# Sixteen tokens of a dense expert block moved to the gathers, and the gathers dealt over all rows

## The chip, the cores and the metric

The kernel runs on 1 core of one Trainium2 chip. The metric is the device time of one execution in microseconds (us), as the median of several runs. The engines are called PE (TensorE matmul; PEld is its weight load), DVE (VectorE), ACT (ScalarE), POOL (GpSimd) and SP (SyncE, which here only issues DMAs).

## The reference

One transformer layer over 512 tokens of width 1024: an adaptive norm, a token mixer (two linear-attention branches), a second norm, and then an expert layer that is most of the time here. Cut to that layer:

```
q   = (xb @ wq).reshape(P, 8, 2, 128)               # P = 128 tokens of a block
sc  = einsum('phzd,hznd->phzn', q, subkeys)         # 2 x 128 keys per head
sv, si = top_k(sc, 16); top_s, top_c = top_k(sums of the 16 x 16 pairs, 16)
experts = si0 * 128 + si1 at top_c                  # 16 of 16384 experts per head
gate = softmax(top_s)
ue, ve = u_tab[experts], v_tab[experts]             # 8 heads x 16 = 128 experts a token
act = gelu(einsum('pd,phkd->phk', xb, ue)) * gate
out = einsum('phk,phkd->pd', act, ve)
```

There are 16384 experts, with a u row and a v row of 1024 floats each, and every token uses 128 of them.

## The kernel before

The 512 tokens are four blocks of 128. **Blocks 0 to 2 go the dense way.** The experts are cut into 128 rows of 128. For each row `i`, `scores(i)` loads 128 x 1024 words of u (`raw<-in_ut`), splits them into a rounded high part `whi` (ACT) and a rest `wlo` (DVE), and multiplies all 384 tokens with them on PE: 8 slices of the width x 3 products = 24 matmuls into the bank `hg`, each over `ND` = 384 token columns (`dhi`, `dlo`). ACT takes the gelu (`ga`). `value_parts(i)` loads and splits the v row (`raw<-in_uv`), multiplies `ga` with the gates of this row (`g`, read back from the DRAM tensor `gd`) and splits the product into `ah` (ACT) and `al` (DVE). `value_sum` adds the row to the three blocks' sums `y` in PSUM: 3 blocks x 2 halves x 3 products = 18 matmuls over 512 columns.

The first 32 rows' scores (`AHEAD`) are taken early, while the gates are still being made, and wait in the DRAM tensor `sd`; they come back as `gr`. So in `dense()` a row under 29 has 18 matmuls, and a later one 42, since it makes the scores of row `i + LEAD` as well.

**Gates.** `route()` takes a block's top 16 of 16 (DVE). `scatter(b, ...)` turns the choices into the dense matrix `gd`, 16 tokens in a turn of its loop over `q`: POOL and DVE make one-hot rows `oj` and `oi`, ACT multiplies gates in, PE multiplies `oj` by `oi` per token (128x128 matmuls, `gd<-oi,oj`), and ACT copies four tokens' results from PSUM into `stage`, one word per token at steps of 16 words.

**Block 3 goes the gathered way.** `gather_block` runs 128 steps; step `c` has POOL issue one indirect DMA that fetches, for each of the 128 tokens, the u and v row of its `c`-th expert (1 MB, five buffers `rows`). DVE takes the dot product with `h2g` (one 128x1024 operation), ACT the gelu, DVE multiplies the gate in and adds the v rows to `acc` (another 128x1024 operation). The steps are dealt among the rows: `run(dense(), ga_)` takes a step of `gather_all()` at each yield of `dense()`. `gather_all()` first ends the route of block 3, so the first yields go to it.

The program is written in this order, and a scheduler in the build settles the order on each engine; engines and the SP queue then work strictly in that order. `back_norm` is the norm ahead of the routes of blocks 2 and 3; its `sink` has POOL copy block 2's columns into `dhi` and `dlo`, PE transpose block 3's, and ACT copy them to `h2g`.

Of the kernel before, what the change touches and what calls it, by code (L numbers as in the profile page):

```python
# [45 lines left out]
NGS = 5  # L46
NST = 4
ADA = (12, 2)
ND = 384
AHEAD = 32  # L50
LEAD = 3
RING = 6
# [14 lines left out]
def mixer_peer_kernel(ctx: ExitStack, tc: tile.TileContext, x, ws, ada, wba, vecs, rows, skt, uv, ut, out, dbg=None):  # L67
# [270 lines left out]
    def pb4(pp, i):  # L338
        return pp[:, i * P:(i + 1) * P]
# [437 lines left out]
    def expert_index(sel):  # L777
        ef = wk.tile([P, PH, 16], F32, tag="lo", name="ef", bufs=1)
        nc.vector.scalar_tensor_tensor(ef, sel[0], 128.0, sel[1], op0=ALU.mult, op1=ALU.add)
        ei = gat.tile([P, PH * 16], I32, tag="ei", name="ei")  # L780
        nc.vector.tensor_copy(ei, f2(ef))
        return ei

# [126 lines left out]

    routes = []
# [5 lines left out]

    def back0(mg):
        hh, hl = dhi[:, :, 0:256], dlo[:, :, 0:256]
        yield from back(0, mg, (dhi[:, :, P:], dlo[:, :, P:]), hh, hl)  # L920
        yield from route(hh, hl, nc.vector, gat, routes)

    xc = load_x(0)
# [72 lines left out]


    den = ctx.enter_context(tc.tile_pool(name="den", bufs=1, **RT))
    h2g = den.tile([P, D], F32, name="h2g")
# [30 lines left out]
    def scatter(b, sel, gate, npool, pool, bufs, tags):  # L1030

        cols = []
        for n, src in (("ti", sel[0]), ("tj", sel[1]), ("tg", gate)):
            pp = bank("tr")
            nc.tensor.transpose(pp[:, 0:P], f2(src), ident)
            c = sct.tile([P, P], F32, tag=n, name=n, bufs=2)
            nc.scalar.copy(c, pp[:, 0:P])
            cols.append(c)
        ti, tj, tg = cols
        for q in range(P // 16):  # L1040
            sg = sct.tile([P, P, 16], F32, tag="stage", name="stage", bufs=2)
            for q4 in range(4):
                pp = bank(tags[q4 % len(tags)])
                t0 = q * 16 + q4 * 4
                oj4 = pool.tile([P, 4, P], F32, tag="oj", name="oj", bufs=bufs)
                oi4 = pool.tile([P, 4, P], F32, tag="oi", name="oi", bufs=bufs)
                for a in range(4):
                    (nc.gpsimd if a < npool else nc.vector).tensor_scalar(oj4[:, a, :], iof, tj[:, t0 + a:t0 + a + 1],  # L1048
                                                                      None, op0=ALU.is_equal)
                if q4 % 2:  # L1050
                    for a in range(4):
                        t = t0 + a
                        nc.vector.tensor_scalar(oi4[:, a, :], iof, ti[:, t:t + 1], tg[:, t:t + 1],
                                                op0=ALU.is_equal, op1=ALU.mult)
                else:
                    nc.vector.tensor_tensor(oi4, iof[:, None, :].to_broadcast([P, 4, P]),
                                            ti[:, t0:t0 + 4, None].to_broadcast([P, 4, P]), op=ALU.is_equal)
                    for a in range(4):
                        nc.scalar.mul(oj4[:, a, :], oj4[:, a, :], tg[:, t0 + a:t0 + a + 1])
                for a in range(4):  # L1060
                    last["pe"] = nc.tensor.matmul(pb4(pp, a), oj4[:, a, :], oi4[:, a, :], start=True, stop=True)  # L1061
                nc.scalar.copy(sg[:, :, q4 * 4:q4 * 4 + 4].rearrange("p i t -> p t i"),
                               pp.rearrange("p (t i) -> p t i", t=4))
            nc.sync.dma_start(gd[:, b * P // 16 + q], sg)
            yield

# [51 lines left out]
    def value_parts(i):  # L1118
        vh, vl = split_load(uv[i * P:(i + 1) * P, D:2 * D])
        if i % 8 == 0:  # L1120
            g = d3.tile([P, ND // 16, 8, 16], F32, tag="g", name="g", bufs=2)
            for b in range(ND // P if i == 0 else 1):
                q = slice(8 * b, 8 * b + 8) if i == 0 else slice(0, ND // 16)
# [9 lines left out]
        ah = d3.tile([P, ND], F32R, tag="ah", name="ah", bufs=2)  # L1133
        al = d3.tile([P, ND], F32R, tag="al", name="al", bufs=2)
        nc.scalar.copy(ah, a)
        last["lo"] = nc.vector.tensor_sub(al, a, ah)  # L1136
        return ah, al, vh, vl

    def value_sum(i, b, hf, ah, al, vh, vl):
# [2 lines left out]
        return mm3(yacc[b][:, d], ah[:, c], al[:, c], vh[:, d], vl[:, d], i == 0, i == P - 1)  # L1142


    def gather_block(h2, gate, ei, d3):
        acc = d3.tile([P, D], F32, tag="acc", name="acc")
        gf = f2(gate)
        r, g = {}, {}
        for c in range(NHK + LAG + 1):
            if c < NHK:  # L1150
# [11 lines left out]
            if 0 <= k < NHK:  # L1162
# [12 lines left out]
    def finish(b, y, gf, d3):  # L1175
# [32 lines left out]

    def gather_all():

        yield from rt
        ei = expert_index(routes[GB][1])
        c_hq.close()
        c_wr.close()
        rows_ = ctx.enter_context(tc.tile_pool(name="rows", bufs=1, reuse_waits="tile"))
        done.append(rows_)
        done.append((yield from gather_block(h2g, routes[GB][0], ei, rows_)))
# [72 lines left out]
```

## Time and profile before

| | |
|---|---|
| time, median of 3 runs | 1899.74 us (1898.4 to 1901.0) |
| the profiled execution's own time | 1898.62 us |
| its span in the trace | 1896.7 us |
| PE busy | 1844.5 us, 97% of the span |
| DVE, ACT, POOL busy | 83%, 51%, 22% |
| DMA traffic | 459.45 MB, 242 GB/s over the span |

The span lies 1.9 us under the execution's own time, and that 1.1 us under the median. "Busy" PE time counts overlapping matmuls, so that the spacing of matmul starts is read from the timeline. The stages in time: mixers to about 600 us, gates and early scores to 934, rows under 29 to 1061, later rows to 1885, then the last norm.

### The profile page before, as it was taken

How to read it: one execution, taken by the hardware profiler on the slowest of the kernel's cores; microseconds unless marked ns; L12 is line 12 of the kernel's file. 1: busy time of each engine (PE TensorE's matmuls, PEld its weight loads, DVE VectorE, ACT ScalarE, POOL GpSimd, SP SyncE). 2: the span in 40 equal slices, each digit the busy share in tenths (PEclk: the TensorE clock that was granted, in tenths of full speed). 3: DMA queues.
4: the chain of work that ended last, by engine and by line, in shares of the span. 5: the costliest groups of instructions: out<-in, count | busy, mean ns of one | idle time of the engine just before them, and what ended most of it. 6: DMA issues, size and time to landing. Idle time of an engine off the chain costs nothing.

```text
span 1896.7 us, 31316 instructions
## 1 busy us (share of the span) xinstructions
PE 1844.5 (97%) x11441; PEld 1708.1 (90%) x11441; DVE 1565.9 (83%) x3422; ACT 972.9 (51%) x1726; POOL 421.5 (22%) x433
## 2 busy tenths in 40 slices
PE   7999989999998999999999999999999999999997
PEld 7999978999998899999977898998998989989896
DVE  6889966989999989999766977887787778887855
ACT  6778634676655788787433333333333333333332
POOL 1000000000000788884100322122211221222100
PEclk9999989999999999999999999999999999999999
DMA  9556734543355556658998998988998998889833
GB/s 321 187 169 198 234 113 156 162 136 95 123 163 175 183 166 211 212 193 265 312 317 256 369 359 307 335 296 310 313 324 300 327 323 289 324 303 331 297 123 111
DMA packets 160521, 459.45 MB, mean 242 GB/s; under 512 B 12528, under 2 KB 78192, under 8 KB 140912
## 3 DMA queue, kind: packets, MB, share of 16 engines
q1 hardware_dynamic: 141936, 323.23, 51.7%
q0 software_dynamic: 18432, 134.23, 18.7%
q8 instruction: 90, 1.47, 0.3%
q14 instruction: 63, 0.52, 0.1%
HBM read 420.71 MB, written 36.70 MB: 241 GB/s over the span
## 4 chain that ended last, share of the span: by engine, by line
PE 91%; ACT 3%; DMA 2%; DVE 2%; POOL 1%; issue 1%; SPq 0%; DVEq 0%; POOLq 0%; ACTq 0%
PE hg L208 9%; PE hg L209 9%; PE hg L207 9%; PE y L208 9%; PE y L209 9%; PE y L207 9%; PE pj L207 8%; PE pj L208 8%; PE pj L209 8%; PE gd L1061 3%; PE hg L543 1%; POOL oj L1048 1%; PE gd L453 1%; PE gd L447 1%; PE pj L1061 1%; DMA adaw<-in_ada 1%
## 5 line engine op out<-in xcount | busy, mean ns | idle before, releaser
L1014 DVE TENSOR_TENSOR wlo<-raw,whi 128x1024 fp32r<-128x1024 f32 x256 | 313.3, 1224 | 124.4 <-ACT whi L1013 124.3
L1013 ACT CAST whi<-raw 128x1024 fp32r<-128x1024 f32 x256 | 267.8, 1046 | 246.4 <-PE y L209 224.4
L209 PE MATMUL hg<-dhi,whi 128*128 128x384 f32 x1024 | 347.9, 340 | 0.0
L207 PE MATMUL hg<-dlo,whi 128*128 128x384 f32 x1024 | 347.9, 340 | 0.0
L208 PE MATMUL hg<-dhi,wlo 128*128 128x384 f32 x1024 | 347.7, 340 | 0.0
L1152 POOL DMA_INDIRECT rows<-in_uv,ei x128 | 167.0, 1304 | 739.4 <-DVE acc L1160 573.1
L208 PE MATMUL y<-whi,al 128*128 128x512 f32 x768 | 304.8, 397 | 1.9 <-DVE al L1136 1.8
L209 PE MATMUL y<-whi,ah 128*128 128x512 f32 x768 | 304.4, 396 | 0.0
L207 PE MATMUL y<-wlo,ah 128*128 128x512 f32 x768 | 295.8, 397 | 0.0
L1048 POOL TENSOR_SCALAR oj<-iof,tj 128x128 f32<-128x128 f32 x256 | 218.7, 871 | 49.7 <-PE gd L1061 32.6
L203 DVE TENSOR_TENSOR wlo<-raw,whi 128x1024 fp32r<-128x1024 f32 x160 | 195.2, 1221 | 31.0 <-ACT whi L202 30.7
L202 ACT CAST whi<-raw 128x1024 fp32r<-128x1024 f32 x160 | 167.3, 1048 | 89.9 <-PE pj L209 62.4
L1027 ACT ACTIVATE ga<-hg 128x384 f32<-128x384 f32 x128 | 63.0, 493 | 276.6 <-PE hg L209 276.4
L208 PEld LDWEIGHTS hg<-dhi,wlo 128*128 128x128 f32 x1024 | 192.2, 188 | 4.2
L207 PEld LDWEIGHTS hg<-dlo,whi 128*128 128x128 f32 x1024 | 192.2, 188 | 4.1
L209 PEld LDWEIGHTS hg<-dhi,whi 128*128 128x128 f32 x1024 | 192.2, 188 | 0.1
L208 PEld LDWEIGHTS y<-whi,al 128*128 128x128 f32 x768 | 144.6, 188 | 35.0 <-DVE al L1136 4.4
L209 PEld LDWEIGHTS y<-whi,ah 128*128 128x128 f32 x768 | 144.5, 188 | 34.6
L207 PEld LDWEIGHTS y<-wlo,ah 128*128 128x128 f32 x768 | 144.6, 188 | 32.0 <-issue 1.0
L1165 DVE SCALAR_TENSOR_TENSOR rows<-rows,h2g 128x1024 f32<-128x1024 f32 x128 | 153.8, 1220 | 0.4 <-DMA rows<-in_uv,ei 0.4
L207 PE MATMUL pj<-wlo,hh 128*128 128x256 f32 x448 | 128.9, 288 | 5.0 <-ACT gsig L627 2.1
L209 PE MATMUL pj<-whi,hh 128*128 128x256 f32 x448 | 128.1, 286 | 0.0
(748 smaller groups left out, 3875.4 us busy)
## 6 DMA issues: line engine op xcount, KB each, us to landing
raw<-in_ws SPq DMA_DIRECT2D x160, 512.0 KB, 3.8
raw<-in_ut SPq DMA_DIRECT2D x128, 512.0 KB, 5.0
raw<-in_uv SPq DMA_DIRECT2D x128, 512.0 KB, 6.5
adaw<-in_ada SPq DMA_DIRECT2D x48, 512.0 KB, 5.2
gd<-stage SPq DMA_DIRECT2D x24, 1024.0 KB, 4.8
g<-gd SPq DMA_DIRECT2D x15, 1536.0 KB, 12.6
sd<-ga SPq DMA_DIRECT2D x32, 192.0 KB, 4.1
gr<-sd SPq DMA_DIRECT2D x32, 192.0 KB, 5.5
```

The source lines that it names most:

```text
L202: nc.scalar.copy(hi, w)
L203: nc.vector.tensor_sub(lo, w, hi)
L207: nc.tensor.matmul(o, lh, rl, start=start, stop=False, **kw)
L208: nc.tensor.matmul(o, ll, rh, start=False, stop=False, **kw)
L209: return nc.tensor.matmul(o, lh, rh, start=False, stop=stop, **kw)
L1013: nc.scalar.copy(hi, w)
L1014: nc.vector.tensor_sub(lo, w, hi)
L1027: nc.scalar.activation(a, o[:, :ND], AF.Gelu)
L1048: (nc.gpsimd if a < npool else nc.vector).tensor_scalar(oj4[:, a, :], iof, tj[:, t0 + a:t0 + a + 1], None, op0=ALU.is_equal)
L1061: last["pe"] = nc.tensor.matmul(pb4(pp, a), oj4[:, a, :], oi4[:, a, :], start=True, stop=True)
L1152: nc.gpsimd.indirect_dma_start(out=r[c], out_offset=None, in_=uv, in_offset=bass.IndirectOffsetOnAxis(ap=ei[:, c:c + 1], axis=0))
L1165: dot = nc.vector.scalar_tensor_tensor(u, u, 1.0, h2, op0=ALU.mult, op1=ALU.mult, accum_out=s)
```

## The change

`ND` becomes 368: the last 16 tokens of block 2 leave the dense matmuls of the scores, the gelu, the gates (`scatter` of block 2 makes 7 turns instead of 8) and `sd`, `gr`, `g`, `ga`. In `ah` and `al` their 16 columns are zeros that are set once, so the 18 value matmuls keep their shape. The 16 tokens x 128 experts are gathered instead: 2048 pairs are spread over 128 partitions as 8 groups of 16 tokens, so that 16 more gather steps do them. For this `sink` makes a tile `xr` that repeats the 16 tokens' columns 8 times (POOL), transposes it (PE) and copies it to `h2x` (ACT); 16 small DMAs on SP spread the expert numbers (`eix`) and gates (`gx`); and after the 16 steps four matmuls with `pick_x` (a matrix of ones and zeros) add the eight groups' sums `accx` into block 2's `y`.

The copy of `scatter` into `stage` now writes runs of four words and reads PSUM at steps of 128 words. The route of block 3 ends ahead of the first row, and the gather steps are dealt from row 1 on: one at every odd row under 29, then one or two at each row, three extra in seven rows (before: from row 20 on, one extra in three rows).

```diff
-ND = 384
+NX = 16
+NG = P // NX
+ND = 384 - NX
...
             if p:
-                nc.gpsimd.tensor_copy(dhi[:, c, 2 * P:], hh[:, c, 0:P])
-                nc.gpsimd.tensor_copy(dlo[:, c, 2 * P:], hl[:, c, 0:P])
+                nc.gpsimd.tensor_copy(dhi[:, c, 2 * P:], hh[:, c, 0:P - NX])
+                nc.gpsimd.tensor_copy(dlo[:, c, 2 * P:], hl[:, c, 0:P - NX])
+                xr_ = thp.tile([P, 2, P], F32, tag="xr", name="xr", bufs=1)
+                nc.gpsimd.tensor_copy(xr_.rearrange("p a (g t) -> p a g t", t=NX),
+                                      h32[:, :, None, P - NX:P].to_broadcast([P, 2, NG, NX]))
                 pp = bank("hg")
                 for a in range(2):
                     nc.tensor.transpose(pb4(pp, a), h32[:, a, P:], ident)
-                nc.scalar.copy(h2[:, j * 256:(j + 1) * 256], pp[:, 0:256])
+                    nc.tensor.transpose(pb4(pp, 2 + a), xr_[:, a, :], ident)
+                for n in range(2):
+                    nc.scalar.copy(h2[n][:, j * 256:(j + 1) * 256], pp[:, n * 256:(n + 1) * 256])
...
-        for q in range(P // 16):
+        for q in range((P - NX if b == GB - 1 else P) // 16):
...
-                nc.scalar.copy(sg[:, :, q4 * 4:q4 * 4 + 4].rearrange("p i t -> p t i"),
-                               pp.rearrange("p (t i) -> p t i", t=4))
+                nc.scalar.copy(sg[:, :, q4 * 4:q4 * 4 + 4], pp.rearrange("p (t i) -> p i t", t=4))
...
+    for dst, src in ((eix, expert_index(routes[GB - 1][1])), (gx, f2(routes[GB - 1][0]))):
+        for g in range(NG):
+            nc.sync.dma_start(dst[g * NX:(g + 1) * NX, :], src[P - NX:P, g * NX:(g + 1) * NX])
     run(first)
-    run(gates(2, NP[1], hold, 4, ("pj", "gd", "pj", "pj")))
+    run(gates(2, NP[1], hold, 4, ("pj", "gd", "pj", "pj")), rt)
+    run(rt)
...
-            if i >= 20 or i % 2:
+            if i >= AHEAD - LEAD or i % 2:
                 yield
-            if i >= AHEAD - LEAD and i % 3 == 0:
+            if i >= AHEAD - LEAD and i % 7 in (0, 2, 5):
                 yield
...
-        yield from rt
-        ei = expert_index(routes[GB][1])
...
+        x = yield from gather(h2g[1], gx, eix, NX, "accx")
+        hi = st.tile([P, D], F32R, tag="whi", name="whi")
+        lo = st.tile([P, D], F32R, tag="wlo", name="wlo")
+        nc.scalar.copy(hi, x)
+        nc.vector.tensor_sub(lo, x, hi)
+        for hf in range(2):
+            d = slice(hf * 512, hf * 512 + 512)
+            for t in (lo, hi):
+                nc.tensor.matmul(yacc[GB - 1][:, d], pick_x, t[:, d], start=False, stop=False)
+        done.append((yield from gather(h2g[0], f2(routes[GB][0]), ei, NHK, "acc")))
```

Two places show how instructions move. The first is POOL at the norm ahead of the routes (`back_norm`), whose copies stand among the one-hot rows `oj` of the gates. Before:

```order
L126 TENSOR_TENSOR rsn<-rs,mhalf 128x2
L1048 TENSOR_SCALAR oj<-iof,tj 128x128 x9
L903 COPY dhi<-thi 128x2x128
L1048 TENSOR_SCALAR oj<-iof,tj 128x128 x3
L904 COPY dlo<-tlo 128x2x128
L1048 TENSOR_SCALAR oj<-iof,tj 128x128 x3
L903 COPY dhi<-thi 128x2x128
L904 COPY dlo<-tlo 128x2x128
L903 COPY dhi<-thi 128x2x128
```

The same place with the change (L908 is the new copy):

```order
L128 TENSOR_TENSOR rsn<-rs,mhalf 128x2
L1055 TENSOR_SCALAR oj<-iof,tj 128x128 x9
L908 COPY xr<-h_8224 128x256
L905 COPY dhi<-thi 128x2x112
L1055 TENSOR_SCALAR oj<-iof,tj 128x128 x3
L906 COPY dlo<-tlo 128x2x112
L1055 TENSOR_SCALAR oj<-iof,tj 128x128 x3
L905 COPY dhi<-thi 128x2x112
L908 COPY xr<-h_8247 128x256
L906 COPY dlo<-tlo 128x2x112
L1055 TENSOR_SCALAR oj<-iof,tj 128x128 x6
```

Between one `xr` and the next there now stand six `oj`, and `xr` has one buffer. The second place is DVE in the rows under 29, where a dot product of a gather has its first operand from `rows`. Before, the first dot product comes behind the 23rd `al`:

```order
L1014 TENSOR_TENSOR wlo<-raw,whi 128x1024
L1132 TENSOR_TENSOR gr<-gr,g 128x384
L1136 TENSOR_TENSOR al<-gr,ah 128x384
L1165 SCALAR_TENSOR_TENSOR rows,gs__12642<-rows,h2g 128x1024
L1132 TENSOR_TENSOR gr<-gr,g 128x384
L1014 TENSOR_TENSOR wlo<-raw,whi 128x1024
```

With the change the first one comes behind the eighth `al`, and this is the piece around the fourth:

```order
L1159 TENSOR_TENSOR al_11846<-gr,ah_11845 128x368
L1188 SCALAR_TENSOR_TENSOR rows,gs__12319<-rows,h2x 128x1024
L1021 TENSOR_TENSOR wlo<-raw,whi 128x1024
L1156 TENSOR_TENSOR gr<-gr,g 128x368
L1193 TENSOR_TENSOR gg__12321<-gg__12321,gx 128x1
L152 TENSOR_SCALAR adac<-adaw,cond 128x512
L1183 SCALAR_TENSOR_TENSOR accx<-rows,gg__12321,accx 128x1024
L1156 TENSOR_TENSOR gr<-gr,g 128x368
L158 SCALAR_TENSOR_TENSOR adac<-adaw,cond,adac 128x512
L1159 TENSOR_TENSOR al_11844<-gr,ah_11843 128x368
```

From there on every second `al` has one gather step beside it, through all rows under 29; before, from the 23rd on, every `al` had one. By the end of the order the last dot product stands behind the 125th `al` (before: the 120th).

## Rows read from the trace of the kernel before

**Rows 1.** The page, first part: busy time, share of the span, instructions.

```profile
PE 1844.5 (97%) x11441; PEld 1708.1 (90%) x11441; DVE 1565.9 (83%) x3422; ACT 972.9 (51%) x1726; POOL 421.5 (22%) x433
```

**Rows 2.** Windows by stage: busy time of each engine, PEclk, DMA share, GB/s.

```profile
600.00:680.00 80.00, 72.61 (x527) 67.77 (x525) 71.64 (x154) 54.95 (x109) 56.92 (x70) 0.94 0.49 161
680.00:900.00 220.00, 218.03 (x1577) 215.47 (x1576) 209.61 (x788) 176.83 (x327) 166.10 (x198) 1.00 0.66 219
1060.00:1100.00 40.00, 40.00 (x198) 35.67 (x197) 38.12 (x56) 15.35 (x27) 14.59 (x10) 1.00 1.03 397
1100.00:1800.00 700.00, 700.00 (x3482) 631.86 (x3481) 558.34 (x775) 251.12 (x443) 138.77 (x108) 1.00 0.88 315
```

**Rows 3.** Timeline of PE in a later row: start, duration, instruction.

```profile
1301.64 0.33 PE L207 MATMUL hg<-dlo,whi 128*128 128x384 f32 x1
...
1305.88 0.39 PE L207 MATMUL y<-wlo,ah 128*128 128x512 f32 x1
...
1310.08 0.34 PE L207 MATMUL hg<-dlo,whi 128*128 128x384 f32 x1
```

**Rows 4.** Timeline of PE elsewhere: 33 matmuls of 256 columns, and 128-column ones.

```profile
103.36 0.28 PE L207 MATMUL pj<-hl,whi 128*128 128x256 f32 x1
...
107.32 0.28 PE L207 MATMUL pj<-hl,whi 128*128 128x256 f32 x1
...
805.68 1.28 PE L1061 MATMUL gd<-oi,oj 128*128 128x128 f32 x10
```

**Rows 5.** Groups by line and form, PEld and DVE, 1050 to 1800 us.

```profile
L208 PEld LDWEIGHTS hg<-dhi,wlo 128*128 128x128 f32 x697 | 130.8, 188 | 3.8
...
L1014 DVE TENSOR_TENSOR wlo<-raw,whi 128x1024 fp32r<-128x1024 f32 x179 | 219.1, 1224 | 91.8 <-ACT whi L1013 91.8
L1165 DVE SCALAR_TENSOR_TENSOR rows<-rows,h2g 128x1024 f32<-128x1024 f32 x121 | 145.3, 1220 | 0.4 <-DMA rows<-in_uv,ei 0.4
...
L1132 DVE TENSOR_TENSOR ga<-ga,g 128x384 f32<-128x384 f32 x87 | 48.5, 557 | 43.0 <-ACT ga L1027 42.8
L1136 DVE TENSOR_TENSOR al<-ga,ah 128x384 fp32r<-128x384 f32 x86 | 47.5, 552 | 5.4 <-ACT ah L1135 5.4
...
L1160 DVE SCALAR_TENSOR_TENSOR acc<-rows,gg__13464,acc 128x1024 f32<-128x1024 f32 x1 | 1.3, 1287 | 0.0
```

**Rows 6.** Groups by line, gates and norm: ACT in 600 to 900, POOL in 640 to 700.

```profile
L1062 ACT COPY stage<-gd 128x512 f32<-128x512 f32 x72 | 76.0, 1073 | 12.0 <-PE gd L1061 11.9
...
L675 ACT COPY qt<-pj 128x512 f32<-128x512 f32 x8 | 4.7, 591 | 2.0 <-PE pj L209 2.0
...
L1048 POOL TENSOR_SCALAR oj<-iof,tj 128x128 f32<-128x128 f32 x58 | 51.0, 895 | 6.1 <-PE gd L1061 6.1
L904 POOL CAST dlo<-tlo 128x256 fp32r<-128x256 f32 x4 | 2.3, 563 | 0.0
```

**Rows 7.** One line, L1061: what the scatter's matmuls waited for (us, times).

```profile
  ACT oj L1059: 13.2, 21
  POOL oj L1048: 3.3, 6
```

**Rows 8.** The tile `y`, 927 to 1062: its matmuls and their wait (us, times).

```profile
L207 PE MATMUL y<-wlo,ah x177: 391/397/798, 934.1 to 1061.6; 128*128 128x512 f32 x177
...
  DVE al L1136: 5.9, 9
```

**Rows 9.** DMA, 925 to 1060: packets and rate, gathers issued.

```profile
DMA packets 20818, 40.97 MB, mean 303 GB/s; under 512 B 1333, under 2 KB 14388, under 8 KB 19654
...
rows<-in_uv,ei POOLq DMA_INDIRECT x10, 8.9
```

**Rows 10.** DMA, 1100 to 1800: the gathers' queue, and their count.

```profile
q0 software_dynamic: 15864, 115.47, 43.8%
...
rows<-in_uv,ei POOLq DMA_INDIRECT x108, 8.3
```

**Rows 11.** The chain that ended last, at the last rows.

```profile
1875.94 0.25 PE y L209
...
1877.37 0.51 PE y L208
```

More of the change, by code (lines that the diff above doesn't have):

```diff
@@ L779, in expert_index @@
         nc.vector.scalar_tensor_tensor(ef, sel[0], 128.0, sel[1], op0=ALU.mult, op1=ALU.add)
-        ei = gat.tile([P, PH * 16], I32, tag="ei", name="ei")
+        ei = gat.tile([P, PH * 16], I32, tag="ei", name="ei", bufs=2)
         nc.vector.tensor_copy(ei, f2(ef))
@@ L919, in back0 @@
         hh, hl = dhi[:, :, 0:256], dlo[:, :, 0:256]
-        yield from back(0, mg, (dhi[:, :, P:], dlo[:, :, P:]), hh, hl)
+        yield from back(0, mg, (dhi[:, :, ND - 256:], dlo[:, :, ND - 256:]), hh, hl)
         yield from route(hh, hl, nc.vector, gat, routes)
@@ L998, in mixer_peer_kernel @@
     den = ctx.enter_context(tc.tile_pool(name="den", bufs=1, **RT))
-    h2g = den.tile([P, D], F32, name="h2g")
+    h2g = [den.tile([P, D], F32, name=n) for n in ("h2g", "h2x")]
     c_th = ctx.enter_context(ExitStack())
@@ L1098, in mixer_peer_kernel @@
         next(first, None)
+    eix = gat.tile([P, NX], I32, name="eix")
+    gx = gat.tile([P, NX], F32, name="gx")
+    for dst, src in ((eix, expert_index(routes[GB - 1][1])), (gx, f2(routes[GB - 1][0]))):
+        for g in range(NG):
+            nc.sync.dma_start(dst[g * NX:(g + 1) * NX, :], src[P - NX:P, g * NX:(g + 1) * NX])
     run(first)
-    run(gates(2, NP[1], hold, 4, ("pj", "gd", "pj", "pj")))
+    run(gates(2, NP[1], hold, 4, ("pj", "gd", "pj", "pj")), rt)
+    run(rt)
+    ei = expert_index(routes[GB][1])
     run(ahead)
     c_hd.close()
+    c_hq.close()
+    c_wr.close()
     c_sc.close()
@@ L1108, in mixer_peer_kernel @@
     psv = ctx.enter_context(tc.tile_pool(name="psv", bufs=1, reuse_waits="tile", space=PSUM))
-    yacc = [psv.tile([P, D], F32, name=f"y{b}") for b in range(ND // P)]
+    yacc = [psv.tile([P, D], F32, name=f"y{b}") for b in range(GB)]
+    s32 = d3.tile([P, P], F32, name="s32")
+    nc.vector.memset(s32, 0.0)
+    nc.vector.tensor_reduce(s32[:, P - NX:], ident.rearrange("p (g t) -> p t g", g=NG), axis=AX.X, op=ALU.add)
+    pick_x = d3.tile([P, P], F32R, name="pick_x")
+    nc.vector.tensor_copy(pick_x, s32)
+    ahl = [[d3.tile([P, GB * P], F32R, name=f"{n}{k}") for n in ("ah", "al")] for k in range(2)]
+    for t in ahl[0] + ahl[1]:
+        nc.vector.tensor_copy(t[:, ND:], s32[:, 0:NX])
     gtile = {}
@@ L1121, in value_parts @@
             g = d3.tile([P, ND // 16, 8, 16], F32, tag="g", name="g", bufs=2)
-            for b in range(ND // P if i == 0 else 1):
-                q = slice(8 * b, 8 * b + 8) if i == 0 else slice(0, ND // 16)
+            for b in range(GB if i == 0 else 1):
+                q = slice(8 * b, min(8 * b + 8, ND // 16)) if i == 0 else slice(0, ND // 16)
                 nc.sync.dma_start(g[:, q], gd[:, q, i:i + 8, :])
@@ L1132, in value_parts @@
         nc.vector.tensor_mul(a3, a3, gtile[0][:, :, i % 8, :])
[L1133 to L1136, printed above, removed]
+        ah, al = ahl[i % 2]
+        nc.scalar.copy(ah[:, 0:ND], a)
+        last["lo"] = nc.vector.tensor_sub(al[:, 0:ND], a, ah[:, 0:ND])
         return ah, al, vh, vl
@@ L1142, in value_sum, with gather @@
         return mm3(yacc[b][:, d], ah[:, c], al[:, c], vh[:, d], vl[:, d], i == 0, i == P - 1)
-    def gather_block(h2, gate, ei, d3):
-        acc = d3.tile([P, D], F32, tag="acc", name="acc")
-        gf = f2(gate)
+    def gather(h2, gf, ei, steps, name):
+        acc = d3.tile([P, D], F32, name=name)
         r, g = {}, {}
-        for c in range(NHK + LAG + 1):
-            if c < NHK:
+        for c in range(steps + LAG + 1):
+            if c < steps:
                 r[c] = d3.tile([P, 2 * D], F32, tag="rows", name="rows", bufs=NROWS)
@@ L1161, in gather_block @@
             k = c - LAG
-            if 0 <= k < NHK:
+            if 0 <= k < steps:
                 s = sm.tile([P, 1], F32, tag="gs_", name="gs_", bufs=4)
@@ L1173, in gather_block, with finish @@
         return acc
-    def finish(b, y, gf, d3):
+    def finish(b, y, gf):
         xb = st.tile([P, D], F32, tag="raw", name="xb")
@@ L1194, in dense @@
             v = value_parts(i)
-            for b in range(ND // P):
+            for b in range(GB):
                 for hf in range(2):
@@ L1209, in gather_all @@
     def gather_all():
-        yield from rt
-        ei = expert_index(routes[GB][1])
[L1213 to L1217, printed above, removed]
+        x = yield from gather(h2g[1], gx, eix, NX, "accx")
[8 more added lines that the diff above has]
+        done.append((yield from gather(h2g[0], f2(routes[GB][0]), ei, NHK, "acc")))
     ga_ = gather_all()
@@ L1221, in mixer_peer_kernel @@
     run(ga_)
-    rows_, yg_ = done
-    gf = rows_.tile([P, 2 * D], F32, tag="rows", name="gf", bufs=NROWS)
+    gf = d3.tile([P, 2 * D], F32, tag="rows", name="gf", bufs=NROWS)
     nc.sync.dma_start(gf[:, 0:D], g2d)
@@ L1226, in mixer_peer_kernel @@
     ends = [(i, value_parts(i)) for i in range(P - NEND, P)]
-    finish(GB, yg_, gf, rows_)
+    finish(GB, done[0], gf)
     end = None
-    for b in range(ND // P):
+    for b in range(GB):
         for hf in range(2):
@@ L1233, in mixer_peer_kernel @@
                     end = value_sum(i, b, hf, *v)
-        finish(b, yacc[b], gf, rows_)
+        finish(b, yacc[b], gf)
 def layout(inp):
```

## Prediction

> **What bounds the kernel now.** I read the page's first part, then the windows by stage, then the timeline of PE, then the waits of single lines. PE is busy for 97% of the span and DVE for 83% [rows 1]. A share over a whole span decides nothing, so the stages come next [rows 2]: from 680 to 1800 us PE is busy throughout but for 2 us in the gates and some microseconds in the rows under 29, with its clock at 1.00, and only from 600 to 680, around the norm ahead of the routes, does it stand at 72.6 of 80 us. DVE is at 80% in the later rows (558 of 700 us) and at 95% both in the gates and in the short stretch from 1060 to 1100, where PE stays full all the same. So a nanosecond off a matmul is a nanosecond off the span in most of the program, as long as no other engine takes over.
>
> What a matmul costs is the distance from one start to the next, not its duration. In a later row, 24 score matmuls take 1301.64 to 1305.88, 176.7 ns each, and the 18 value matmuls of 512 columns take 4.20 us, 233.3 ns each [rows 3]. 33 matmuls of 256 columns take 3.96 us, 120.0 ns each [rows 4]. From 256 to 384 columns that is 0.443 ns a column, from 384 to 512 it is 0.442: one straight line through all three widths.
>
> **The change, part by part.**
>
> *Narrower scores.* 128 rows x 24 = 3072 matmuls lose 16 columns each. On the line that is 16 x 0.442 = 7.1 ns each, 169.6 ns instead of 176.7, and 3072 x 7.1 ns = 21.8 us. All of them stand where PE is full: the early scores in the gates, the others in the later rows. A later row shrinks from 8.44 to 8.27 us. The bounds are 0 (if the weight load, 188 ns long [rows 5], set the pace) and 21.8; I take 21.8, since the 256-column matmuls, with weight loads of the same size, already run at 120 ns.
>
> *One turn of the gates less.* 16 matmuls of 128 columns go, at 1.28 us for ten, less the last one's drain some 0.11 each [rows 4]: -1.8 us of PE, and eight `oj` on POOL (895 ns each [rows 6]).
>
> *More on PE.* Four matmuls with `pick_x` at 233 ns and eight transposes at 0.11: +1.8 us. The narrower `ga`, `ah`, `al` and their DVE work gain 4% of 0.55 us each [rows 5], beside PE, so nothing.
>
> *The norm's copies.* On POOL each `xr` is a new 128x256 copy with a repeating read. No row shows one; the plain casts of that size take 563 ns [rows 6]. From one `xr` to the next POOL now has six `oj`, the copies and `xr` itself: 6 x 0.895 + about 1.4 = 6.8 us. On PE, whose order is fixed, the work between the transposes of two `xr` is some 50 matmuls of 256 columns and a few small ones, about 6 us. Three such distances, each 0.8 us short: +2 us. Below, 0 if POOL's `oj` run ahead; above, 3 x 2 = 6 us, if `xr` costs twice the cast.
>
> *The copy into `stage`.* Before, an ACT copy of 512 words takes 1073 ns when it writes single words 16 apart, and 591 ns when it writes them in a row [rows 6]. With runs of four it lies between; 92 copies could save up to 92 x 0.48 = 44 us of ACT, none of it on the path by itself. What the path can gain is what PE waits for ACT's `oj` in the scatter, 13.2 us, and for POOL's, 3.3 [rows 7], most of it ahead of 680 us. A copy ahead of an `oj` in ACT's queue delays it by at most the copy's length, so halving copies might halve the wait, if PE had nothing else late; the norm's chain is late there too. I take -2 us, with 0 and -7 as bounds. [...]
>
> *The gathers.* A step costs DVE a dot product of 1220 ns, an addition of 1287 [rows 5] and two short operations, 2.7 us. 16 more are 43 us of DVE and 16 MB, all beside matmuls. In the later rows DVE has 2 x 1.22 + 0.56 + 0.55 = 3.55 us a row and 10/7 steps, 7.4 of 8.27 us; before it was 4/3 steps, 7.2 of 8.44. One step holds all DMA engines for 0.438 x 700 / 108 = 2.84 us [rows 10]; a row had 0.88 x 8.44 = 7.4 us of them [rows 2] and will have about 7.75 of 8.27, a share of 0.94. From 1060 to 1100 ten gathers in 40 us gave a share of 1.03 at 397 GB/s, and PE stayed full [rows 2]. So this costs nothing; if that cover were gone, each 0.1 us a row is 9.7 us.
>
> *The rows under 29.* They take 934.1 to 1061.6, of which PE waits 5.9 us for `al` [rows 8]: from the 23rd row on each row of 4.2 us (18 x 233 ns) has a step beside it, 2.33 + 2.7 us of DVE. Now there is one step in two rows, 3.7 us a row, from the eighth row on: these waits should go. But the weights of the adaptive norm's last two units (16 products of 128x512, by half of a 128x1024 one [rows 5] about 0.6 us each) fall in the same rows, so DVE comes to nearly 100% there, and the bytes rise: 17 gathers (12 dot products by the 30th `al` in the order, and five buffers) instead of 10 [rows 9], so about 48 MB instead of 41 in 130 us, 370 GB/s. Taken together 0, between -5 and +9.
>
> *The end.* The last two gather steps now stand just ahead of `al` of row 125, and the norm of block 3 (six 128x512 operations of DVE) between the last `al`. Before, PE already waits 1.2 us there for `ah` and `al` of row 127 [rows 11]. +1.5 us, between 0 and +4. The 16 DMAs on SP stand among prefetched loads and cost nothing; if their wait for the gates held SP up, the early scores behind them would wait up to 2 us.
>
> **Sum.** The profiled execution's own 1898.6 (span 1896.7, 1.9 around it) - 21.8 - 1.8 + 1.8 + 2 - 2 + 0 + 1.5 = 1878.3; it lies 1.1 under the median of its runs, so 1879.4, and I say 1879.
>
> **The rivals.**
>
> *The first rows run dry.* 16 steps begin at once, beside loads that already move 303 GB/s [rows 9]. For it: DVE near 100%, in strict order, each step with a landing, a gelu and a buffer to wait for. Against: 397 GB/s and 95% of DVE held PE full for 40 us [rows 2]. At 0.35 us a row over 29 rows: +10, so 1889. [...]
>
> *Faster gates.* The shorter ACT copies shorten the whole chain POOL, ACT, PE around the norm, where PE misses 7.4 of 80 us [rows 2]: -8 more, 1871.
>
> *The width doesn't pay.* If the pace of 176.7 ns were the weight load's and not the columns', the 21.8 us stay: 1901, no change. For it is only the load's 188 ns; against it the straight line.
>
> *Slower: the gathers become the bound of the later rows.* With 94% of DMA and 89% of DVE and two steps in three of seven rows, a step that lands too late stops DVE at its dot product, which stands ahead of the next `al`, and so PE. It decides from 7% more DMA time per gather on: at 10%, a row takes 8.53 us, 97 rows lose 25 us, 1904. Against it are the stretch at 1.03 and a DVE wait for landings of 0.4 us in all [rows 5].
>
> **How the numbers follow.** Sum as it stands 0.62 (1872 to 1886), first rows 0.15, faster gates 0.13, width 0.05, slower 0.05. The time is that of the first, 1879. The range from 1868 to 1892 takes in the bounds of the norm, copy, first rows and end, and leaves out the last two cases and the tails. A measurement of this kernel tells about 0.2%, 3.8 us, from no change. Faster: the first three but for 0.02 of the first rows, 0.88; same: those 0.02 and 0.03 of the width case, 0.05; slower: the gathers' case and the 0.02 of the width case in which the added work shows, 0.07.
>
> **What would show it.** Score matmuls 169 to 170 ns apart; later rows 8.27 us long with PE full; `xr` on POOL under 0.8 us and less than 10 us missing on PE from 600 to 680; the copies into `stage` at 0.6 to 0.8 us; from the first value matmul to that of row 29 at most 127 us; PE's wait at the last `al` under 4 us. I am wrong if the scores stay at 176 ns, if PE shows waits for `al` in later rows, or if the first rows take over 135 us.

## The result and the profile after

The changed kernel takes **1871.95 us** (median of 4 runs, 1871.05 to 1874.78) against 1900.37 for the kernel before in the same runs: a ratio of 0.9847, with a 95% interval of 0.9832 to 0.9861. The forecast was 1879, range 1868 to 1892, faster: right in sign and range, and 7 us too slow.

The profiled execution took 1871.05 us, span 1869.3, so 27.4 us less of span than before. The first part of its page, beside [rows 1]:

```profile
PE 1815.7 (97%) x11421; PEld 1680.2 (90%) x11421; DVE 1595.9 (85%) x3478; ACT 934.9 (50%) x1735; POOL 439.7 (24%) x445
```

Windows by stage of the changed kernel, beside [rows 2], and one short stretch, 998 to 1005 us (columns as there; the third from the right is PE's granted clock):

```profile
600.00:680.00 80.00, 72.96 (x542) 68.12 (x542) 72.31 (x154) 49.73 (x109) 57.24 (x70) 0.96 0.51 169
680.00:900.00 220.00, 219.93 (x1616) 219.69 (x1616) 211.73 (x802) 151.91 (x327) 170.14 (x198) 1.00 0.66 233
...
998.00:1005.00 7.00, 6.53 (x16) 5.12 (x17) 4.28 (x6) 1.78 (x2) 0.00 (x0) 0.52 0.96 330
...
1020.00:1060.00 40.00, 40.00 (x179) 32.88 (x178) 34.10 (x52) 14.31 (x24) 6.33 (x6) 1.00 0.94 335
1060.00:1100.00 40.00, 40.00 (x203) 35.68 (x202) 24.87 (x34) 15.63 (x24) 4.28 (x5) 1.00 0.75 271
1100.00:1800.00 700.00, 700.00 (x3570) 629.54 (x3569) 585.99 (x824) 255.52 (x462) 159.98 (x121) 1.00 0.90 330
```

The reader is to see that PE is as full as before, that DVE (586 of 700 us) and DMA (0.90) have risen in the later rows without stopping it, that ACT lost 25 us in the gates, and that around 1000 us the clock fell to near half.

Timeline of PE in a later row, beside [rows 3]: 24 score matmuls in 4.02 us.

```profile
1304.35 0.33 PE L209 MATMUL hg<-dlo,whi 128*128 128x368 f32 x1
...
1308.37 0.39 PE L209 MATMUL y<-wlo,ah 128*128 128x512 f32 x1
```

That is 167.5 ns each, where 176.7 stood before and 169.6 was forecast. With these starts the span is cut into four stretches (in us; every kernel of the study is in it, from the starts of its value matmuls `y`):

| kernel | to first `y` | rows under 29 | row 29 to last `y` | last `y` to end |
|---|---|---|---|---|
| before | 934.1 | 127.0 | 823.6 | 11.9 |
| changed | 921.9 | 130.8 | 804.2 | 12.4 |
| ladder of widths (on before) | 932.4 | 130.7 | 807.9 | 11.9 |
| old copy | 925.6 | 131.5 | 804.2 | 12.4 |
| new copy only (on before) | 934.9 | 128.7 | 823.6 | 12.0 |
| pitch 384 | 924.5 | 128.0 | 806.1 | 12.4 |
| late deal | 925.1 | 135.4 | 806.1 | 12.4 |
| no extra steps | 919.0 | 135.7 | 804.2 | 12.1 |
| scores 384 wide | 932.9 | 132.2 | 817.6 | 12.0 |
| 32 tokens | 913.5 | 131.5 | 825.9 | 12.8 |
| 32 tokens, other rows | 914.3 | 132.6 | 819.8 | 12.9 |
| units early | 925.8 | 138.6 | 804.2 | 12.3 |
| no steps at rows 13 to 19 | 922.3 | 124.7 | 804.2 | 12.5 |

The third stretch is the same to 0.1 us in five kernels that share its order and widths; the first two are where kernels differ by accident of their waits, and a difference of 2 or 3 us there in one execution says little.

Groups of ACT in the changed kernel, 600 to 935 us, beside [rows 6]: the copy into `stage`.

```profile
L1069 ACT COPY stage<-gd 128x512 f32<-128x512 f32 x71 | 41.0, 580 | 13.1 <-PE gd L1068 12.6
```

Groups of POOL in the changed kernel, 600 to 900 us; L908 is the new copy.

```profile
L1055 POOL TENSOR_SCALAR oj<-iof,tj 128x128 f32<-128x128 f32 x248 | 215.4, 885 | 42.3 <-PE gd L1068 30.2 <-ACT tj L1044 9.0 <-PE pj L1068 1.0
...
L908 POOL COPY xr<-h 128x256 f32<-128x256 f32 x4 | 2.8, 698 | 0.0
```

One line of the changed kernel, L1068: the gates' matmuls, and what they waited for (us, times), beside [rows 7].

```profile
L1068 PE MATMUL gd<-oi,oj x568: 270/275/581, 615.4 to 870.6; 128*128 128x128 f32 x190
...
L1068 PE MATMUL pj<-oi,oj x168: 270/275/276, 828.8 to 873.7; 128*128 128x128 f32 x168
...
  ACT oj L1066: 9.0, 12
  POOL oj L1055: 2.5, 6
```

The copies run at 580 ns, the price of a copy that is contiguous on both sides (591), though they read PSUM at steps of 128 words and write runs of four: neither costs time here, and the forecast's "between" 591 and 1073 was too high.

### The profile page after: what moved, and what is told of

The parts are those of the page before. It is cut to its first block, busy times and chain, and to the rows that moved or that the text cites. A ratio compares the mean times of both kernels' runs of the same rounds, so it can differ in the third digit from the quotient of the medians.

```text
span 1869.3 us, 31386 instructions
## 1 busy us (share of the span) xinstructions
PE 1815.7 (97%) x11421; PEld 1680.2 (90%) x11421; DVE 1595.9 (85%) x3478; ACT 934.9 (50%) x1735; POOL 439.7 (24%) x445
## 4 chain that ended last, share of the span: by engine, by line
PE 50%; DVE 1%; ACT 0%; issue 0%; DVEq 0%; POOLq 0%; POOL 0%; ACTq 0%
PE y L211 10%; PE y L210 10%; PE y L209 10%; PE hg L209 7%; PE hg L211 7%; PE hg L210 7%; DVE t L1212 0%; ACT ah L1158 0%; DVE al L1159 0%; DVE accx L1183 0%; DVE t L1205 0%; DVE t L1206 0%; DVE wlo L1021 0%; DVE rows L1188 0%; DVE gr L1156 0%
## 5 line engine op out<-in xcount | busy, mean ns | idle before, releaser
L209 PE MATMUL hg<-dlo,whi 128*128 128x368 f32 x1024 | 339.7, 332 | 2.2 <-ACT ga L1034 2.2
L211 PE MATMUL hg<-dhi,whi 128*128 128x368 f32 x1024 | 338.8, 331 | 0.0
L210 PE MATMUL hg<-dhi,wlo 128*128 128x368 f32 x1024 | 338.4, 330 | 0.0
L1034 ACT ACTIVATE ga<-hg 128x368 f32<-128x368 f32 x128 | 60.8, 476 | 263.1 <-PE hg L211 256.4
```

What stands on the lines that cost most here:

```text
L209: nc.tensor.matmul(o, lh, rl, start=start, stop=False, **kw)
L210: nc.tensor.matmul(o, ll, rh, start=False, stop=False, **kw)
L211: return nc.tensor.matmul(o, lh, rh, start=False, stop=stop, **kw)
L1034: nc.scalar.activation(a, o[:, :ND], AF.Gelu)
```

## The experiments

**What a column is worth: a ladder of widths on the kernel before.** Of each row's 24 score matmuls, those of the last seven slices get a width that depends on the row; beyond it, columns keep only the first slice's products.

```diff
+WIDTHS = (384, 382, 380, 376, 372, 368, 352, 320)
-            mm3(o[:, :ND], ..., dhi[:, kk, :], dlo[:, kk, :], kk == 0, kk == KD - 1)
+            n = ND if kk == 0 else WIDTHS[i % 8]
+            mm3(o[:, :n], ..., dhi[:, kk, :n], dlo[:, kk, :n], kk == 0, kk == KD - 1)
```

> The kernel before, but of each row's 24 score matmuls only the first covers 384 columns; the other 23 cover a width that goes round over the rows: 384, 382, 380, 376, 372, 368, 352, 320 (so the scores of up to 64 tokens of block 2 lack seven eighths of their sum). The tiles keep their pitch of 384 columns. Straight line (0.442 ns a column, as predicted): 176.7, 175.8, 174.9, 173.1, 171.4, 169.6, 162.5, 148.4 ns from start to start. Rival, a step at 384 (the changed kernel shows about 167 ns at 368): some width just under 384 already falls to 173 or less, 368 lies at 167, and the line goes on below it. Rival, the pitch of the operand in SBUF: here, at the old pitch, 368 stays at 169.6 or more.

Measured: 1884.9 us in its one execution. The first slice has three products, so 21 matmuls of a row are narrowed and not 23. Mean distances from one start to the next in the later rows: 176.6 ns at 384; 173.9, 173.8 and 173.4 at 382, 380 and 376; 170.4 at 372; 173.1 at 368; 162.9 at 352; 146.6 at 320. So narrower is cheaper, without a step that would bring 368 to 167, but the line is rough by some 3 ns: 382 columns already save 2.7 ns, and 368 cost more than 372. From row 29 on the kernel gained 15.7 us; the distances, 7.8 ns in the mean, make 96 x 21 x 7.8 = 15.7, all of it. The early scores brought 1.7 us, and 3.7 were lost in the rows under 29, which the ladder doesn't touch.

**The copy, taken back and taken alone.** The first is the changed kernel with the old copy, the second the kernel before with the new one:

```diff
-                nc.scalar.copy(sg[:, :, q4 * 4:q4 * 4 + 4], pp.rearrange("p (t i) -> p i t", t=4))
+                nc.scalar.copy(sg[:, :, q4 * 4:q4 * 4 + 4].rearrange("p i t -> p t i"),
+                               pp.rearrange("p (t i) -> p t i", t=4))
```

> The changed kernel with the old copy into stage (single words 16 apart) put back, nothing else. If the copy is worth what was predicted, 2 us: 1874. If it is the source of most of what the gates gained beyond the narrower scores (some 5 us): 1877 to 1880, with ACT copies of 1.07 us and PE's waits for ACT's oj back at about 13 us. If ACT was never on the path: 1872.

> The kernel before with the new copy into stage alone. Copy worth 2 us: 1898. Copy worth 5 us or more: 1895 or less, with the copies at 0.58 us instead of 1.07. ACT never on the path: 1900.

Measured: taken back, 1872.88 us (0.9839 of before, 0.981 to 0.9868); alone, 1896.99 (0.9976, 0.9961 to 0.9991). Groups of ACT from 600 to 935 us, with the old copy in the changed kernel:

```profile
L1069 ACT COPY stage<-gd 128x512 f32<-128x512 f32 x71 | 75.4, 1071 | 11.3 <-PE gd L1068 11.2
```

The same group with the new copy in the kernel before:

```profile
L1062 ACT COPY stage<-gd 128x512 f32<-128x512 f32 x72 | 41.4, 581 | 15.1 <-PE gd L1061 14.8
```

Halving the copy is worth about 1 us on the changed kernel, which its interval doesn't tell from nothing, and some 4 us on the kernel before (2 to 7 by its interval). The profiled execution of the latter, 1901.06 us, is the slowest of its ten, so its trace doesn't show where they come from. Of some 44 us of ACT time (92 copies of 0.48 us) little reaches the span: ACT only waits longer ahead of `oj`, for POOL and DVE. Here is that group of ACT with the old copy in the changed kernel, and in the changed kernel itself:

```profile
L1066 ACT ACTIVATE oj<-oj,tg 128x128 f32<-128x128 f32 x184 | 66.7, 402 | 21.9 <-POOL oj L1055 15.2 <-DVE oj L1055 6.4
```

```profile
L1066 ACT ACTIVATE oj<-oj,tg 128x128 f32<-128x128 f32 x184 | 69.0, 401 | 44.7 <-POOL oj L1055 33.8 <-DVE oj L1055 10.6
```

**The pitch.** The changed kernel with `dhi` and `dlo` 384 apart, as before the change:

```diff
-    dhi = per.tile([P, KD, ND], F32R, name="dhi")
+    dhi = per.tile([P, KD, 384], F32R, name="dhi")[:, :, 0:ND]
```

> The changed kernel with dhi and dlo laid out at a pitch of 384 columns again, of which 368 are used. If the width alone sets the pace, the scores stay at 167 ns and the time at 1872. If the pitch of the operand does part of it, the scores go to 169.6 ns and the time to about 1880.

Measured: 1873.66 us, 0.9855 (0.9827 to 0.9883); distances of 168.9 ns instead of 167.5. The third stretch grew by 1.9 us; the 2304 scores in it make 3.2, and its value matmuls, 233.7 ns apart instead of 234.3, gave 1.1 back. The pitch may be worth a nanosecond a matmul, not more.

**The scores at 384 columns again**, all else as changed, except that `dhi` and `dlo` are 384 wide too and filled to the end (those lines are left out here):

```diff
-            mm3(o[:, :ND], uh[:, c], ul[:, c], dhi[:, kk, :], dlo[:, kk, :], ...)
+            mm3(o[:, :GB * P], uh[:, c], ul[:, c], dhi[:, kk, :], dlo[:, kk, :], ...)
```

> The changed kernel with the scores at 384 columns again (the 16 columns more are computed and not used; everything else as changed). If the width is worth what the spacing measured after the change gives, 3072 x (176.6 - 167.5) ns = 28 us, this is 1900, and all other terms of the sum cancel. By the straight line of the prediction, 21.8 us, it is 1894, and 6 us come from the copy and the gates. If the width is worth what the ladder of widths returned on the kernel before, about 15 us, it is 1887, and 13 us come from elsewhere.

Measured: 1897.37 us, 0.9983 (0.997 to 0.9996). Its PE timeline in a later row:

```profile
1304.21 0.34 PE L209 MATMUL hg<-dlo,whi 128*128 128x384 f32 x1
...
1308.37 0.39 PE L209 MATMUL y<-wlo,ah 128*128 128x512 f32 x1
```

Without the narrower scores, then, 25 of the 28 us are gone: the width is the change. But 24 matmuls take 4.16 us here, 173.4 ns each, 3 less than the same shape took before the change. So 16 columns with their pitch are worth 5.9 ns in like surroundings, 3072 x 5.9 = 18 us (at the same pitch of 384, against the kernel above, 4.5 ns or 14 us); the other 7 or 8 of the 25 are waits ahead of the first `y` and in the rows under 29.

**Without the 16 extra gather steps**, so that the last 16 tokens of block 2 get no expert sum:

```diff
-        x = yield from gather(h2g[1], gx, eix, NX, "accx")
+        for _ in range(NX + LAG + 1):
+            yield
+        x = h2g[1]
```

> The changed kernel without the 16 extra gather steps (the last 16 tokens of block 2 get no expert sum; their yields stay, so the other steps stand where they stood). The prediction put the steps at nothing: 1872, later rows 8.24 us. If the early steps cost the 3.7 us of the rows under 29, 1868. If the gathers held up the later rows too, rows under 8.24 us and a time below 1865; against that, 18 x 0.2346 + 24 x 0.1675 is 8.24 already.

Measured: 1873.18 us, 0.9862 (0.9845 to 0.988). Taken as a whole the steps cost nothing, as forecast. But the dot products taken out stand beside rows 6 to 30, so that this kernel doesn't test what the closer deal costs the later rows. Rows 16 and 17 no longer stall (4.6 and 4.2 us), yet the rows under 29 took 135.7 us, longer than with the steps: rows 8 and 9 take 9.5 and 6.0 us and row 22 takes 8.4; both stalls wait for an early score on its way back from `sd`. The chain of waits at row 8 (start, duration):

```profile
937.18 17.39 DMA gr<-sd
954.57 0.02 issue
954.59 0.55 DVE gr L1156
```

**The deal of before** (no step ahead of row 20):

```diff
-            if i >= AHEAD - LEAD or i % 2:
+            if i >= 20:
                 yield
-            if i >= AHEAD - LEAD and i % 7 in (0, 2, 5):
+            if i >= AHEAD - LEAD and i % 2 == 0:
```

> The changed kernel, but the gather steps dealt as before the change: none ahead of row 20, one a row from there, two at every even row from 29 on. If the 3.7 us that the rows under 29 lengthened come from the gather steps that now stand beside them, the stretch from the first value matmul to that of row 29 goes back to 127 us and the time to 1868 or 1869. If they are the scatter of one execution, the stretch stays within 127 to 131 us as it likes and the time is 1872. The later rows get 1.5 steps each instead of 1.43: 2 x 1.22 + 0.56 + 0.55 + 1.5 x 2.7 = 7.6 of 8.24 us on DVE, so they should stay at 8.24; if they run dry there, each 0.05 us a row is 5 us, 1877.

Measured: 1874.69 us, 0.986 (0.9844 to 0.9875). Rows 16 and 17, now without a step beside them, take 4.6 and 4.2 us. But the rows under 29 did not go back to 127 us: as before the change the waits for `al` come in the rows from 20 on, and larger (rows 22 and 26 take 6.5 and 11.5 us instead of 4.2). The profiled execution, 1880.8 us, is the longest of its four by 5 us. So this deal exchanges one stall for others; that dealing from row 1 on is better isn't shown, since the two intervals overlap.

**The stall at rows 16 and 17.** In the changed kernel all rows under 29 take 4.2 to 4.9 us, but for row 16 with 8.2 and row 17 with 7.1. PE's timeline there (in brackets its idle time before, and what ended it; L167 is a matmul of the adaptive norm's second unit):

```profile
994.21 0.39 PE L211 MATMUL y<-whi,ah 128*128 128x512 f32 x1
996.27 1.12 PE L167 MATMUL hg<-adac,ones 128*128 128x512 f32 x2 [1.67 <-DVE adac L158]
998.48 0.79 PE L209 MATMUL y<-wlo,ah 128*128 128x512 f32 x1 [1.08 <-DVE wlo L1021]
999.07 0.63 PE L210 MATMUL y<-whi,al 128*128 128x512 f32 x1
999.49 0.63 PE L211 MATMUL y<-whi,ah 128*128 128x512 f32 x1
```

And DVE's timeline beside it: `al` was ready at 991.5; then come a dot product, an addition and two of the unit's products, ahead of `wlo`, which PE wants next. DVE wasn't short of time: it stood idle for 1.93 us ahead of that `al`, waiting for `ah`, for which ACT had waited 3.72 us for PE's value matmuls.

```profile
991.00 0.54 DVE L1159 TENSOR_TENSOR al<-gr,ah 128x368 fp32r<-128x368 f32 x1 [1.93 <-ACT ah L1158]
991.46 1.22 DVE L1188 SCALAR_TENSOR_TENSOR rows<-rows,h2x 128x1024 f32<-128x1024 f32 x1
...
993.16 1.28 DVE L1183 SCALAR_TENSOR_TENSOR accx<-rows,gg__12478,accx 128x1024 f32<-128x1024 f32 x1
994.36 0.74 DVE L158 SCALAR_TENSOR_TENSOR adac<-adaw,cond,adac 128x512 f32<-128x512 f32 x1
...
995.47 0.74 DVE L158 SCALAR_TENSOR_TENSOR adac<-adaw,cond,adac 128x512 f32<-128x512 f32 x1
...
997.20 1.22 DVE L1021 TENSOR_TENSOR wlo<-raw,whi 128x1024 fp32r<-128x1024 f32 x1
```

Two experiments move one of the two sides away. The first puts the units at other rows:

```diff
-            if i in (8, 16):
-                ada_unit(10 + i // 16, pool=d3)
+            if i in (1, 4):
+                ada_unit(10 + i // 4, pool=d3)
```

> The changed kernel with the two units of the adaptive norm's weights at rows 1 and 4 instead of 8 and 16. In the changed kernel rows 16 and 17 take 8.2 and 7.1 us instead of 4.2 each, the second at the lower clock. If that is the unit's products on DVE standing among dot products and additions of the gathers, both rows go back to 4.2, nothing of the kind shows at rows 1 to 6, where DVE has run ahead, and the time is 1865 to 1868. If the stall only moves with the unit, one of rows 1 to 8 takes 8 us and the time stays at 1872. If it has nothing to do with the unit, rows 16 and 17 stay as they are: 1872.

Measured: 1883.45 us, 0.9903 (0.9882 to 0.9923): worse by some 11 us. Rows 16 and 17 are back at 4.2, but rows 1, 2 and 4 take 10.0, 6.8 and 6.8. The stall moved with the unit and grew, though no dot product stands beside these rows (the first comes in row 6). So beside the first rows a unit alone is enough; that DVE has not yet run ahead there is likely, and not shown. What the value matmuls and their weight loads waited for in the rows under 29 (the tile `y`; us, times, PE and PEld added up):

```profile
  DVE al L1159: 8.9, 6
  DVE wlo L1021: 2.3, 3
```

The second leaves the units where they are and deals no step beside the second one:

```diff
-            if i >= AHEAD - LEAD or i % 2:
+            if i >= AHEAD - LEAD or (i % 2 and not 12 < i < 20):
                 yield
-            if i >= AHEAD - LEAD and i % 7 in (0, 2, 5):
+            if i >= AHEAD - LEAD and (i % 7 in (0, 2, 5) or i in (32, 39, 46, 53)):
```

> The changed kernel with no gather step dealt at rows 13 to 19; the four steps left out there come as second steps at rows 32, 39, 46 and 53. If the stall at rows 16 and 17 needs both the unit's products and a gather step beside them, both rows go back to 4.2 to 4.7 us and the time is 1865 to 1868, unless the four steps cost something in the later rows (two rows with three steps' worth of DVE, 3.4 + 2 x 2.7 = 8.8 us, would lose half a us each). If it is the unit alone, the rows stay and the time is 1872.

Measured: **1866.22 us**, 0.9817 (0.9793 to 0.984), the best kernel of the study; four of its five runs (1865.2 to 1866.9) lie below all runs of the changed kernel, the fifth at 1872.9. The intervals of the two ratios overlap a little (0.9832 to 0.9861 for the changed kernel); where the time went is plain from the rows. Rows 16 and 17 take 4.7 and 4.5 us, the rows under 29 together 124.7 instead of 130.8, and the later rows are unchanged. Its window of the same 7 us, with the clock at 1.00:

```profile
998.00:1005.00 7.00, 7.00 (x31) 5.64 (x30) 5.36 (x8) 2.69 (x5) 0.00 (x0) 1.00 0.93 321
```

And what its value matmuls and their weight loads waited for up to row 29 (the tile `y`; us, times):

```profile
  issue: 0.5, 2
  DVE wlo L1021: 0.3, 1
```

**Twice as many tokens**, 32 instead of 16, in two deals of the steps over the later rows (the second kernel has the residues 0, 2, 4, 6):

```diff
-NX = 16
+NX = 32
-            if i >= AHEAD - LEAD or i % 2:
+            if i >= AHEAD - LEAD - 1 or i % 2:
-            if i >= AHEAD - LEAD and i % 7 in (0, 2, 5):
+            if i >= AHEAD - LEAD and i % 7 in (1, 3, 4, 6):
```

> 32 tokens moved instead of 16 (scores 352 wide, 32 extra gather steps, block 2's gates in six turns), with one step at each odd row under 29 and 1.57 a row later. If matmuls set the time, a later row is 18 x 0.234 + 24 x 0.160 to 0.163 = 8.06 to 8.13 us and the time 1849 to 1858. Beside it DVE has 2 x 1.22 + 1.06 + 1.57 x 2.7 = 7.7 us, 95%, and DMA about 3.4 + 1.57 x 2.84 = 7.8 us, 97%. If the gathers become the bound at that share, rows stay at 8.25 or grow, PE waits for al, and the time is 1872 or more.

> The kernel with 32 tokens moved, with the second steps at other rows (residues 0, 2, 4 and 6 of 7 instead of 1, 3, 4 and 6), nothing else. In the first version 14 of the later rows took 9 to 16 us, where the splits of loaded rows on ACT stood behind the gelu of a gather step that waited for its dot product. If that is an accident of the order, other rows stall or fewer, and the time lies anywhere from 1850 to 1890. If it is the load of the engines and queues, the same 20 us of PE are missing from 1100 to 1800 and the time is 1880 to 1886.

Measured: 1883.13 us, 0.9906 (0.9892 to 0.9919), and with the other rows 1880.34, 0.9879 (0.9858 to 0.99). The scores ran at 162.9 ns and most later rows took 8.1 us, as by the first theory; but from 1100 to 1800 PE missed 20 us in the one and 18 in the other, in single rows of 9 to 16 us. Window of the first:

```profile
1100.00:1800.00 700.00, 679.55 (x3450) 606.12 (x3450) 577.09 (x833) 253.82 (x455) 202.95 (x126) 0.99 0.90 332
```

DVE is at 82% and DMA at 0.90, as in the changed kernel: neither is full. ACT's timeline at one stall of the first shows what holds PE up:

```profile
1337.66 0.49 ACT L1158 CAST ah<-ga 128x352 fp32r<-128x352 f32 x1 [3.65 <-PE y L211]
1339.96 0.20 ACT L1192 ACTIVATE gg__15448<-gs__15446 128x1 f32<-128x1 f32 x1 [1.80 <-DVE rows L1188]
1341.58 0.46 ACT L1034 ACTIVATE ga<-hg 128x352 f32<-128x352 f32 x1 [1.42 <-PE hg L211]
1341.94 3.88 ACT L1020 CAST whi<-raw 128x1024 fp32r<-128x1024 f32 x4
```

Four splits `whi` stand behind the gelu `gg` of a gather step, which waits for its dot product, and that stands behind `al`; and behind the gelu `ga` of the scores, which waits for PE. ACT stands idle for 3 us (1.80 ahead of `gg`, 1.42 ahead of `ga`) and then runs the four splits without a gap; DVE follows with four `wlo`, and PE's next value matmul, which needs the first of them, comes 2.75 us late. At this stall the strict order holds PE up, and not the bytes. Landings alone don't explain the loss either: in these 700 us ACT waits 25.3 us for loads of u in the first kernel and 1.3 in the second, and the second lost nearly as much.

The rows differ only in part. Over 10 us take rows 39, 41, 63, 79, 95 and 111 in the first kernel and 39, 79, 95 and 103 in the second. All but 41 stand two rows behind a row in which SP issues a load of `g` (row 37 and every eighth from there; behind 45, 53, 69 and 85 neither kernel stalls so). What that load has to do with it is not settled, and neither is what share the number of steps has and what share their order.

## Why the prediction was right, and what it mis-sized

The terms, in us, each against its measurement:

| step | forecast | measured |
|---|---|---|
| narrower scores | -21.8 | -26.9 |
| one turn of gates less | -1.8 | -3.6 |
| norm's copies, transposes, waits of gates and early scores | 2 - 2 + 0.9 = +0.9 | -2.7 |
| four `pick_x` matmuls, rest of the later rows | +0.9 | +1.7 |
| rows under 29 | 0 | +3.7 |
| end | +1.5 | +0.4 |
| sum | -20.3 | -27.4 |

The first two are counts times distances; the third and fourth are what is left of the first and third stretch.

**Scores.** The mechanism held: the pace is the columns' (167.5 ns at 368; in the ladder 162.9 at 352 and 146.6 at 320) and not the weight load's, which is 188 ns long in both kernels, and PE stays full at the shorter row (8.24 us, forecast 8.27). The size was off. In the later rows 96 x 24 x 9.1 ns make 21.0 us, and the 768 early ones, 129.7 us in all instead of 135.6, make 5.9 (each without its waits). Not all of this is the width: put back, it returned 5.9 ns a matmul, 18 us, less than the forecast's 21.8, and the other 9 came with some part of the change that the prediction had no term for. That the two errors add up to a gain that lies inside the range is luck. The slope from three widths of the kernel before carried over to the changed kernel only within about 3 ns a matmul (384 columns: 176.7 ns there, 173.4 with the change's other parts), and times 3072 that is 9 us. Why the same 384 columns took 176.6 ns before and 173.4 with the change's other parts stays open: neither the new copy (176.6 with it alone) nor the pitch (384 in both) is it. The distance is nearly the same in every later row of a kernel (176.3 to 176.7 ns before, 167.5 to 167.9 with the change, over more than 90 rows each), so it isn't a passing disturbance.

**One turn less.** The step that failed by its count: a turn has 16 tokens, but each token's product shows as two matmuls in the trace. `gd` and `pj` of L1061 were 576 + 192 = 768 in all, and are 568 + 168 = 736 now, so 32 of some 0.11 us go, not 16. The row of ten in 1.28 us [rows 4] has the price right; the number of matmuls was taken from the code.

**Norm.** `xr` took 698 ns, between the cast and the bound, and no wait came of it: from 600 to 680 PE is at 72.96 us against 72.61. The +2 was a chain worked out from means that the trace did not bear out.

**Copy.** Forecast 0 to -7 and taken as -2: about -1 by the kernel with the old copy. The rest went into ACT's idle time ahead of `oj`, which grew from 21.9 us with the old copy to 44.7 with the new one. The bound was read too wide: the 13.2 us of [rows 7] add up the waits of PE and of its weight loads, which lie side by side. PE's own idle time ahead of these matmuls is a third of that, here for the larger group from 600 to 935 us, before and with the change:

```profile
L1061 PE MATMUL gd<-oi,oj 128*128 128x128 f32 x576 | 84.6, 284 | 6.6 <-ACT oj L1059 2.9 <-DVE oi L1056 2.2 <-POOL oj L1048 1.1
```

```profile
L1068 PE MATMUL gd<-oi,oj 128*128 128x128 f32 x568 | 82.0, 283 | 5.9 <-ACT oj L1066 2.5 <-DVE oi L1063 2.2 <-POOL oj L1055 0.5
```

**Gathers.** Right at nothing: DMA 0.90 (forecast 0.94), DVE 586 of 700 us, no wait for `al` in the later rows, and the kernel without the steps is no faster. In the rival that has the gathers become the bound, the 10% were put on all of a row's DMA time (7.75 x 1.1 = 8.53); on the gathers alone, 10/7 x 2.84 = 4.1 us of it, they give 8.16 us, still under the row's 8.27.

**Rows under 29.** The sign that the prediction gave, at most 127 us, was not met. Both halves of the step were there. PE's waits for `al` from row 22 on went, as said, though the 5.9 us of [rows 8] again add up PE and its weight loads: PE's own were 1.8, and rows 22 to 28 were 3.0 us longer than seven of 4.2. The unit's products together with the gathers held PE up, and that half was taken as cancelling the first; it cost 6 us (rows 16 and 17, 15.4 us where 9.3 stand without steps beside the unit), of which about 2.9 are 15 matmuls at the lower clock, 0.43 us apart instead of 0.23. It came by the order on DVE and not, as said, by a DVE near 100%: over these rows DVE was busy 106.2 of 130.7 us, 81%. By the kernel without steps at rows 13 to 19 the term without it would have been -2.3. The rival "first rows run dry" had the place, but not the reach (one pair of rows, not 29); its 0.35 us a row was an estimate that no run shows, and the other 27 rows took 4.2 to 4.9 us. The bytes came to 46.03 MB from 913 to 1052 us, 331 GB/s (forecast 48 MB, 370 GB/s); nothing in the chain through row 16 waits for a landing, so these rows don't show where the bytes would set the pace. "Faster gates" had the time, 1871, for the wrong reason.

**End.** PE waits 1.2 us at the last `al`, as before the change.

## What to carry to other kernels

Count instructions in the trace and not in the code, and take a saving that is thousands of equal matmuls times a few nanoseconds with the spread of those nanoseconds as its range: here it was the whole result and most of the error. Where two background jobs share an engine that works in strict order, look at the few rows in which both fall together and keep them apart there; that was worth 6 us, while DVE's average share over these rows, 81%, said nothing about it. Moving more work to idle engines paid here with 16 tokens (1871.95 us) and no further with 32 (1883.13 and 1880.34): at a stall its small dependent steps stood ahead of the loads' splits in ACT's queue, with DVE at 82% and DMA at 0.90.

## What the runs showed of the hardware

A gap of PE cost more than itself in one kernel and not in another. In the changed kernel, after the stretch from 994.6 to 998.5 us with two matmuls in it, the granted clock was 0.52 in the mean from 998 to 1005 us, and the value matmuls came 0.43 us apart instead of 0.23 until 1004.6. In the kernel with the wide pitch, with a like gap from 997.2 to 1001.1 us and two matmuls in it, the same row took 8.3 us and the one behind it 4.3, and the granted clock stayed at 1.00 from 990 to 1010; none of its value matmuls with `whi` up to 1066 us took more than 0.40 us, where the changed kernel's took up to 0.63.

ACT's copies that read 512 columns of PSUM in steps of 128 words and write four words together took 580 ns, copies contiguous on both sides 591; with single words written 16 apart they took 1071 ns, in the same kernel with the old copy.
